# Finer first loads, and two row scales and the MLP norm's squares computed another way, in a one-core hybrid attention layer

## The chip, the core and the metric

The kernel runs on one core of one Trainium2 chip. The metric is the device time of one execution in microseconds; lower is better. The time before is the median of three runs.

## The reference, cut to what matters

One layer over 512 tokens of width 1024 in float32; `rms` is the RMS norm of a token's row times a gain.

```
h    = rms(x);  proj = h @ W_in            # fox q,k,v,f (8 heads of 64), hgrn q,f,i,g (4 heads of 128)
A    = fox_attention(q, k, v, log_sigmoid(f + bias))          # causal, blocks of 128 queries
B    = rms(hgrn2_chunkwise(silu(gq), gf, gi, lb)) * silu(gg)  # gated recurrence
x   += concat(A, B) @ W_out
x   += cross_attention(rms(x), rms(mem)) @ W_xo               # 4 heads, 256 memory tokens
x   += square(relu(rms(x) @ W1)) @ W2                         # width 4096
out  = rms(x)
```

The change touches the row scale 1/sqrt(mean(x^2) + eps) of the first norm and of the MLP's norm, the first loads, and the order in which one projection of the attention is finished.

## The kernel before

**Layout.** Activations are kept feature-major: 8 chunks of 128 features, each with 512 token columns. Every large product is done as three matmuls per chunk of 128: an operand is split into a high part (rounded) and a low part (the rest), and high x high, low x high, high x low are added in PSUM (L240 to L242 in `gemm_fm`). For a panel of weights, ACT rounds the high half (L175, tiles `wh..`) and DVE subtracts it to get the low half (L179, tiles `wl..`); a panel of 256 columns has two halves a and b of four chunks each.

**Row scales are applied late.** The products use the unscaled x times the gain; the scale of a token (a column in this layout) is multiplied in when a product leaves PSUM. For that a vector with one scale per token, held as 128 partitions x 4, must become `rbc`, a tile in which all 128 partitions hold the same 512 scales. Before, PE does it with 4 matmuls of the broadcast vector against the identity (`rbc`, L520 for the first norm, L1500 for the MLP's, 4 of 128 columns; the trace counts two passes of each, 8), and DVE copies the result from PSUM (L522, L1501).

**The first projection.** SP loads x (`xt`, L328) and the first panel (`wr0a`, `wr0b`, L195) in turn, two chunks of weights per load. PE passes the time with matmuls on zeros (`warm`, L352, 7 of them, and L447, 4 more), transposes the chunks of x (`xn`, L412), ACT and DVE write the high and low parts (`hn_hi` L415, `hn_lo` L418), and PE adds up two output tiles gf0 and gf1 (L458 for chunk 0, then L240 to L242). Between the chunks a table `jobs` sets what else ACT and DVE do: splits of weights (`first`, `second`), copies of the transposed x to be parked in DRAM (`x_park`, tiles `xT`), and sums of squares by rows (`x_sq`, L435 on ACT, L437 on DVE, results `ms`). ACT's and DVE's order is written out by hand here; elsewhere a scheduler sets the order on ACT, DVE, POOL and SP from due times, and PE's order is always the order of the code. Then come gf2 and gf3 from panel 1, the four gates `sg` (L544), and the four products gq (L572).

**Fill.** During the recurrence and the attention, `fill` feeds pieces of later projections to PE between the dependent steps, by a credit per step. `proj0` is the first of the attention's projections: its product `pk` becomes `ks` (L765) and the low part `kl` (L770), which the first scores `ps` (L929, L930) read. The recurrence has four state steps c = 0 to 3; `k_T(0)` (L823) copies the transposed keys `kt` from PSUM, which the state products `pst` (L841) read.

**The MLP's norm.** `residual` (L1062 to L1070) produces the new x chunk by chunk; for each chunk POOL squares it and adds it to `ssq`, and after the last chunk PE multiplies `ssq` with ones (`pm`, L1080), DVE and POOL make the scale (L1082, L361, L364), PE spreads it (`rbc`, L1500). `to_tok` transposes the new x back to token rows (`ht` L1162, copies to `acc` L1166, L1168), for the last residual. The MLP's first products u (L240 to L242, tiles u000, u001, u010, u011 in group 0) are scaled by `ur` (L1298), squared (L1301) and summed. POOL also adds rows by accumulating DMAs (`wq`, L1238).

Of the kernel before, what the change touches and what calls it, by code (L numbers as in the profile page):

```python
# [30 lines left out]
GF = 5  # L31
WARM, WARM2 = 7, 4
P1, P2, P3, P4, PW = 20, 20, 20, 10, -20
# [9 lines left out]
def emit(  # L43
# [138 lines left out]

    def load_unit(name, spec, ks, parts=1, between=None):
# [6 lines left out]
        nk = uk // parts  # L190
        splits = []
        for q in range(parts):
            qs, src_ks = slice(q * nk, (q + 1) * nk), slice(ks.start + q * nk, ks.start + (q + 1) * nk)
            for sl, src in spec:
                nc.sync.dma_start(raw_[:, qs, sl], src[:, src_ks, :])  # L195
            if between is not None:
                between(q)
            splits.append(split_of(hi[:, qs, :], lo[:, qs, :], raw_[:, qs, :]))
        return (hi, lo), splits

    def load_next(parts=2, between=None):

        i = len(stream)
        if i >= len(specs):
            return []
        units, splits = [], []
        uk = specs[i][0][1].shape[1] // 2
        for n in range(2):
            note = None if between is None else (lambda q, n=n: between(n * parts // 2 + q))
            unit, some = load_unit(f"{i}{'ab'[n]}", specs[i], slice(n * uk, (n + 1) * uk), parts // 2, note)  # L210
# [118 lines left out]

    def more_x(q):  # L330
        if q == 0:
            load_x(P, P)
        if q < 3:
            load_x((q + 1) * WT)

# [106 lines left out]
    with tc.manual_schedule(engines={mybir.EngineType.Activation, mybir.EngineType.DVE}):  # L442
# [26 lines left out]
        def l_soft():  # L469
# [43 lines left out]
        rstd_of(ms0, NT, "r0", r0)  # L513

        fb = cp.tile([P, FH], F32, name="fb")
        gp.tensor_copy(fb[:, 0:NT], r0)
        gp.dma_start(fb, fox_f_bias[0].partition_broadcast(P))
# [6 lines left out]
        gfps.append(mm("gf3"))  # L524
        gf3 = gemm_fm(gfps[3], wt1, P, hn_hi, hn_lo)
# [27 lines left out]
        x_park(6)  # L553
        gate(0)
        gate(1)
        x_park(5)
        third[0]()
        third[1]()
        run_now(gf3)
        gate(2)  # L560
        for h in range(3):
# [267 lines left out]
    for c in range(NT):  # L829
# [24 lines left out]
        with ahead(P1):  # L854
# [184 lines left out]
    def residual(src_hi, src_lo, g, dst_hi, dst_lo, name, ssq, order, nlast, after=None):  # L1039
# [16 lines left out]
        def rest():  # L1056
            for c in range(KC):
# [6 lines left out]
                ve.scalar_tensor_tensor(dst_lo[:, c, :], hc, g[:, c : c + 1], f(dst_hi[:, c, :]), op0=ALU.mult, op1=ALU.subtract)  # L1064
                if c == 0:
# [93 lines left out]
    def to_tok(c):  # L1159
# [3 lines left out]
        for tb in range(NT):  # L1163
            d, s_ = acc[tb][:, c * P : (c + 1) * P], ps[:, tb * P : (tb + 1) * P]
            if tb % 2 == 0:
                ac.activation(d, s_, AF.Copy)  # L1166
            else:
                ve.tensor_copy(d, s_)  # L1168

    fill.add(x_proj(1), "xq1")  # L1170
    fill.run(2.0)
    for h in range(4):
        if 0 < h < 3:
            fill.add(x_proj(h + 1), f"xq{h + 1}")
        elif h == 3:
            x2_hi, x2_lo = act_tile("x2_hi"), act_tile("x2_lo")
            ssq2 = t2("ssq2")
            early, rest = residual(o_hi, o_lo, g_ff, x2_hi, x2_lo, "xw", ssq2, range(KC), 2, to_tok)
            fill.add(early())
# [324 lines left out]
    for up in ups:  # L1504
        square(*up)
# [44 lines left out]
```

## Time and profile before

| | |
|---|---|
| median of 3 runs | 769.62 us (769.13 to 769.89) |
| the profiled execution's own time | 769.81 us |
| its span in the trace | 768.1 us, 1.7 us less |
| busy PE | 757.7 us, 99% of the span |
| busy DVE, ACT, POOL | 525.1, 368.2, 191.5 us |

The span is what the trace covers; the rest of the profiled execution's time, 1.7 us, lies around it. PE's clock was granted in full, on average 0.999. PE's matmuls stand back to back, so that a stretch of PE work is read best from the chain of work that ended last, where each piece is the time to the next piece.

### The profile page before, as it was taken

What the parts mean: (1) busy time and instruction counts of PE and PEld (TensorE: products, weight loads), DVE (VectorE), ACT (ScalarE), POOL (GpSimd) and SP (SyncE); (2) the same over time, 40 slices, a digit from 0 to 9 for tenths busy, and PEclk for the clock granted to TensorE, in tenths of its full rate; (3) what the DMA queues carried; (4) which work ended last, traced back from release to release, by engine and by line L of the source; (5) the groups of instructions that cost most, each with busy time, mean ns of one, the idle gap of its engine ahead of it and who ended that gap; (6) DMA issues with size and microseconds to landing.
All of it is one profiled execution on the core that took longest, in us unless ns stands there. A gap on an engine that the chain in (4) does not pass through costs nothing.

```text
span 768.1 us, 10959 instructions
## 1 busy us (share of the span) xinstructions
PE 757.7 (99%) x4085; PEld 637.6 (83%) x4085; DVE 525.1 (68%) x847; ACT 368.2 (48%) x618; POOL 191.5 (25%) x264
## 2 busy tenths in 40 slices
PE   8999999999999999999999999999999999999996
PEld 6889888888889988888888888888888888888885
DVE  5747862686867656555548656949596877777696
ACT  5655555665766433244444244435353534342553
POOL 7207531532432125310016510100001010101123
PEclk9999999999999999999999999999999999999999
DMA  8541333231643542222113596565748475758602
GB/s 247 192 124 58 97 84 111 83 98 68 193 158 117 165 135 85 82 92 75 55 55 105 204 257 143 145 161 173 183 146 203 138 191 144 192 137 216 140 1 109
DMA packets 78870, 103.01 MB, mean 134 GB/s; under 512 B 4657, under 2 KB 56410, under 8 KB 78818
## 3 DMA queue, kind: packets, MB, share of 16 engines
q1 hardware_dynamic: 69266, 76.61, 31.2%
q0 software_dynamic: 8960, 24.67, 15.2%
q10 hardware_dynamic: 592, 1.05, 0.4%
q8 instruction: 32, 0.52, 0.3%
q14 instruction: 20, 0.16, 0.1%
HBM read 89.71 MB, written 4.21 MB: 122 GB/s over the span
## 4 chain that ended last, share of the span: by engine, by line
PE 96%; DVE 1%; DMA 1%; POOL 1%; issue 0%; ACT 0%; SPq 0%; POOLq 0%; ACTq 0%
PE u L242 8%; PE u L240 8%; PE u L241 8%; PE U L1364 4%; PE U L1362 4%; PE U L1363 4%; PE xq L240 2%; PE xq L241 2%; PE xw L240 2%; PE xq L242 2%; PE xw L241 2%; PE xw L242 2%; PE wo L240 2%; PE Y L1364 2%; PE wo L242 2%; PE Y L1363 2%
## 5 line engine op out<-in xcount | busy, mean ns | idle before, releaser
L179 DVE TENSOR_TENSOR wld<-wq,whd 128x1024 fp32r<-128x1024 f32 x56 | 68.7, 1226 | 25.5 <-ACT whd L175 25.4
L240 PE MATMUL u<-x_hi,whu 128*128 128x512 f32 x192 | 74.7, 389 | 0.0
L241 PE MATMUL u<-x_lo,whu 128*128 128x512 f32 x192 | 74.7, 389 | 0.0
L242 PE MATMUL u<-x_hi,wlu 128*128 128x512 f32 x192 | 74.7, 389 | 0.0
L175 ACT ACTIVATE whd<-wq 128x1024 fp32r<-128x1024 f32 x56 | 58.4, 1054 | 30.4 <-PE u L241 18.4
L175 ACT ACTIVATE whu<-wru 128x1024 fp32r<-128x1024 f32 x24 | 25.3, 1054 | 61.7 <-DMA wru<-in_w_dram 61.7
L1238 POOL DMA_DIRECT2D wq<-in_w_dram x16 | 19.4, 1242 | 129.6 <-DMA wq<-in_w_dram 118.0
L179 DVE TENSOR_TENSOR wlu<-wru,whu 128x1024 fp32r<-128x1024 f32 x24 | 29.5, 1229 | 32.5 <-ACT whu L175 32.5
L1362 PE MATMUL U<-whd,hb 128*128 128x512 f32 x120 | 46.7, 389 | 0.0
L1363 PE MATMUL U<-wld,hb 128*128 128x512 f32 x120 | 46.7, 389 | 0.0
L1364 PE MATMUL U<-whd,hb 128*128 128x512 f32 x120 | 46.7, 389 | 0.0
L1238 POOL DMA_DIRECT2D wq<-wq x16 | 14.1, 879 | 123.4 <-DVE wld L179 86.3
L241 PEld LDWEIGHTS u<-x_lo,whu 128*128 128x128 f32 x192 | 36.0, 188 | 7.5
L242 PEld LDWEIGHTS u<-x_hi,wlu 128*128 128x128 f32 x192 | 36.0, 188 | 7.5
L240 PEld LDWEIGHTS u<-x_hi,whu 128*128 128x128 f32 x192 | 36.0, 188 | 7.4
L920 POOL TENSOR_SCALAR bi<-nF,Ft 128x128 f32<-128x128 f32 (+3 forms) x32 | 19.6, 620 | 58.2 <-PE pt L952 32.0
L1301 ACT ACTIVATE sq<-ur 128x512 f32<-128x512 f32 x32 | 20.0, 627 | 26.5 <-DVE ur L1298 26.5
L1298 DVE SCALAR_TENSOR_TENSOR ur<-u,rbc 128x512 f32<-128x512 f32 x32 | 21.9, 688 | 11.7 <-PE u L242 11.7
L1363 PEld LDWEIGHTS U<-wld,hb 128*128 128x128 f32 x120 | 22.5, 188 | 4.7
L1364 PEld LDWEIGHTS U<-whd,hb 128*128 128x128 f32 x120 | 22.5, 188 | 4.7
L1362 PEld LDWEIGHTS U<-whd,hb 128*128 128x128 f32 x120 | 22.5, 188 | 4.6
L1063 ACT ACTIVATE x_hi<-hT,gv 128x512 fp32r<-128x512 f32 x16 | 11.5, 719 | 29.3 <-DVE hT L1062 29.3
(960 smaller groups left out, 2313.8 us busy)
## 6 DMA issues: line engine op xcount, KB each, us to landing
wq<-in_w_dram SPq DMA_DIRECT2D x40, 512.0 KB, 3.3
wru<-in_w_dram SPq DMA_DIRECT2D x24, 512.0 KB, 6.5
wq<-in_w_dram POOLq DMA_DIRECT2D x16, 512.0 KB, 8.1
wq<-wq POOLq DMA_DIRECT2D x16, 512.0 KB, 4.7
xTd<-xT POOLq DMA_DIRECT2D x4, 512.0 KB, 3.3
nF<-Fd POOLq DMA_DIRECT2D x8, 256.0 KB, 3.7
hT<-xTd POOLq DMA_DIRECT2D x4, 512.0 KB, 3.6
xt<-in_x_dram SPq DMA_DIRECT2D x3, 512.0 KB
```

Of the source, the lines that this page charges most:

```text
L175: ac.activation(hi, raw, AF.Copy)
L179: ve.tensor_tensor(lo, raw, f(hi), ALU.subtract)
L240: te.matmul(ps, wh, hi, start=n_ == 0 and not begun, stop=False)
L241: te.matmul(ps, wh, lo, start=False, stop=False)
L242: te.matmul(ps, wl, hi, start=False, stop=k == order[-1])
L920: gp.tensor_scalar(bi[:, 0:n], fF[h][:, 0:n], -1.0, Ft[:, tb, h : h + 1], op0=ALU.mult, op1=ALU.add)
L1238: gp.dma_start(raw.rearrange("p (k n) -> p k n", k=2), src, accum_op=ALU.add)
L1298: ve.scalar_tensor_tensor(u, ps, 0.0, rbc2, op0=ALU.max, op1=ALU.mult)
L1301: ac.activation(sqs[g, j][:, i, :], u, AF.Square)
L1362: te.matmul(ps, hi, whi[:, k, :], start=begin, stop=False, skip_group_check=True)
L1363: te.matmul(ps, hi, wlo[:, k, :], start=False, stop=False, skip_group_check=True)
L1364: te.matmul(ps, lo, whi[:, k, :], start=False, stop=k == 1, skip_group_check=True)
```

## The change

Five things are changed.

- **First loads.** Chunks 0 to 3 of x and of panel 0 come one chunk per load, alternating; then chunks 4 and 5 of the weights, then of x, and 6 and 7 likewise: 12 loads where there were 9. The matmuls on zeros are 5 and 2 where they were 7 and 4. The table `jobs` is shifted: the second half of the b splits comes one step later, `x_sq(2)` moves behind the last chunk's `hn_lo`.
- **First row scale.** It no longer goes through PE. POOL writes r0 (16 bytes per partition) to a DRAM tile `Rd`, and reads it back to all partitions as one row of 512 (`on_all`); DVE reorders the row into `rbc`. Gates 0 and 1 come after that copy, behind gf3's products. gf3 and gq0 take PSUM tiles from another pool (`tr`), and the load of the bias `fb` is issued later.
- **The recurrence and the attention.** `kt` of step 0 is copied by DVE instead of ACT. `proj0` is finished before state step 3, by `fill.until`.
- **The MLP's norm.** The squares are taken by token rows from `acc`: four ACT squares of 512 columns at chunk 3, and four DVE reductions of 256 columns each at chunks 5 and 7. The 16 POOL squares and additions and PE's `pm` are gone. The scale goes through `Rd` by two DMAs on ACT's queue.
- **The MLP's first group.** All four u come in one loop behind that; u011 takes its bank from another pool.

```diff
-WARM, WARM2 = 7, 4
+WARM, WARM2 = 5, 2
...
+    xs_ = [*(lambda c=c: load_x(c * P, P) for c in range(1, 4)), lambda: None, lambda: load_x(2 * WT), lambda: load_x(3 * WT)]
...
-    first = load_next(4, more_x)
+    first = load_next(((1, 1, 1, 1), (2, 2)), more_x)
...
+    def on_all(q, i, r, dst):
+        q.dma_start(Rd[i].rearrange("(p t) -> p t", t=NT), r)
+        row = t2(f"row{i}")
+        q.dma_start(row, Rd[i].partition_broadcast(P))
+        def here():
+            ve.tensor_copy(dst.rearrange("p (t q) -> p t q", t=NT), row.rearrange("p (q t) -> p t q", t=NT))
+        return here
...
         jobs = (
-            (first[1],),
-            (lambda: x_park(0), lambda: x_park(1), first[2]),
-            (first[3], lambda: second.extend(load_next())),
-            (lambda: x_sq(0), lambda: x_park(3)),
-            (lambda: x_park(2), lambda: second[0]("h"), lambda: x_sq(2)),
-            (lambda: x_sq(1), lambda: second[0]("l"), lambda: x_sq(3)),
+            (first[2], first[3]),
+            (lambda: x_park(0), lambda: x_park(1)),
+            (first[4], lambda: second.extend(load_next())),
+            (first[5], lambda: x_sq(0), lambda: x_park(3)),
+            (lambda: x_park(2), lambda: second[0]("h")),
+            (lambda: x_sq(1), lambda: x_sq(2), lambda: second[0]("l"), lambda: x_sq(3)),
...
-        pb = sc("rbc")
-        for tb in range(NT):
-            te.matmul(pb[:, tb * P : (tb + 1) * P], r0[:, tb : tb + 1].to_broadcast([P, P]), ident, start=True, stop=True)
-        ve.tensor_copy(rbc, pb)
+        rbc_here = on_all(gp, 0, r0, rbc)
...
-        ac.activation(kts[c], pk, AF.Copy)
+        if c == 0:
+            ve.tensor_copy(kts[c], pk)
+        else:
+            ac.activation(kts[c], pk, AF.Copy)
...
+        if c == NT - 2:
+            fill.until("proj0")
...
+        if c == 3:
+            for tb in range(NT):
+                ac.activation(t2(f"ms2j{tb}"), acc[tb][:, 0:S], AF.Square, scale=1.0 / 32.0, accum_out=ms2[c][:, tb : tb + 1])
...
+            ve.tensor_tensor_reduce(out=t2(f"ms2j{c}{tb}")[:, 0 : 2 * P], in0=a, in1=a, scale=1.0 / D, scalar=old, op0=ALU.mult, op1=ALU.add, accum_out=new_)
...
-    ms2 = mean_sq(ssq2, "pm2")
-    r2 = rstd_of(ms2, NT, "r2")
     to_tok(KC - 2)
     to_tok(KC - 1)
-    up1 = next(ups)
-    pb = tr("rbc2")
-    for tb in range(NT):
-        te.matmul(pb[:, tb * P : (tb + 1) * P], r2[:, tb : tb + 1].to_broadcast([P, P]), ident, start=True, stop=True)
-    ve.tensor_copy(rbc2, pb)
-    square(*up0)
-    square(*up1)
-    for up in ups:
+    gp.tensor_tensor(r2, ms2[KC - 1], mhalf[:, 0:NT], op=ALU.pow)
+    on_all(ac, 1, r2, rbc2)()
+    first_adds(0)
+    for up in [up0, *ups]:
         square(*up)
```

The order on DVE at the end of the first projection, first before, then after. The `ISA` rows are the two parts of one sum of squares by rows (`x_sq`); `wl1a` is the low part of the first half of panel 1, which gf2 reads.

```order
L418 SCALAR_TENSOR_TENSOR hn_lo<-xn_309,g_mix,hn_hi 128x512
L437 ISA x0j_319,ms_193<-xt 128x1024
L437 ISA ms_193 128x1
L418 SCALAR_TENSOR_TENSOR hn_lo<-xn_327,g_mix,hn_hi 128x512
L179 TENSOR_TENSOR wl1a<-wr1a,wh1a 128x1024
```

```order
L430 SCALAR_TENSOR_TENSOR hn_lo<-xn_313,g_mix,hn_hi 128x512
L430 SCALAR_TENSOR_TENSOR hn_lo<-xn_329,g_mix,hn_hi 128x512
L449 ISA x0j_338,ms_195<-xt 128x1024
L449 ISA ms_195 128x1
L179 TENSOR_TENSOR wl1a<-wr1a,wh1a 128x1024
```

One sum of squares has moved from ahead of the last chunk's low part to the place between it and `wl1a`.

The order on DVE at the start of the attention, first before, then after. `rec` is the output of a state step of the recurrence, `mx_lo` the low part of a mixed output, `mt` the memory's rows, `ks` and `kl` the attention's first keys.

```order
L179 TENSOR_TENSOR wl11a<-wr11a,wh11a 128x1024
L862 SCALAR_TENSOR_TENSOR rec_1599<-po_1577,hr_1597,gg_826 128x128 x4
L816 SCALAR_TENSOR_TENSOR mx_lo<-pr_1620,gv,mx_hi 128x4x128
L372 TENSOR_TENSOR m1m<-m1m 128x1
L765 TENSOR_TENSOR ks_1633<-pk_1513,rbc 128x512
L374 TENSOR_SCALAR mt_1607<-mt_1607,m1r 128x1024
L179 TENSOR_TENSOR wl11b<-wr11b,wh11b 128x1024
L770 TENSOR_TENSOR kl_1510<-ks_1633,kh_1509 64x512 x2
```

```order
L179 TENSOR_TENSOR wl11a<-wr11a,wh11a 128x1024
L776 TENSOR_TENSOR ks_1577<-pk_1515,rbc 128x512
L179 TENSOR_TENSOR wl11b<-wr11b,wh11b 128x1024
L781 TENSOR_TENSOR kl_1512<-ks_1577,kh_1511 64x512
L827 SCALAR_TENSOR_TENSOR mx_lo<-pr_1589,gv,mx_hi 128x4x128
L781 TENSOR_TENSOR kl_1512<-ks_1577,kh_1511 64x512
L876 SCALAR_TENSOR_TENSOR rec_1642<-po_1620,hr_1640,gg_828 128x128 x4
```

`ks` and `kl` now stand ahead of the last state step's `rec` and of `mt`, where they stood behind both.

The order on ACT at the MLP's norm, first before, then after. `acc` are the token rows of the last two chunks, `wh36a` and `wh36b` the high halves of a weight panel of the MLP, `sq` the squares of the first u.

```order
L1166 ACTIVATE acc_4211<-ht_4541 128x128
L1166 ACTIVATE acc_4211<-ht_4550 128x128
L175 ACTIVATE wh36a<-wr36a 128x1024
L175 ACTIVATE wh36b<-wr36b 128x1024
L1301 ACTIVATE sq_4592<-ur_4590 128x512
```

```order
L1184 ACTIVATE acc_4212<-ht_4526 128x128
L1184 ACTIVATE acc_4212<-ht_4535 128x128
L175 ACTIVATE wh36a<-wr36a 128x1024
L370 DMA Rd<-r_4553 128x4
L372 DMA row_4556<-Rd 128x512
L175 ACTIVATE wh36b<-wr36b 128x1024
L1338 ACTIVATE sq_4650<-ur_4648 128x512
```

The two DMAs of the scale stand between the two halves of panel 36 on ACT, and the second can be issued only when the first has landed.

## Rows read from the trace of the kernel before

**Rows 1.** The page's busy time by engine: us, share of the span, instructions.

```profile
PE 757.7 (99%) x4085; PEld 637.6 (83%) x4085; DVE 525.1 (68%) x847; ACT 368.2 (48%) x618; POOL 191.5 (25%) x264
```

**Rows 2.** All waits of PE: waiting line, releaser, us, times, longest us.

```profile
PE warm L352 <- DVE ones L356: 1.3, 1, 1.3
PE ps L930 <- DVE kl L770: 1.1, 2, 0.6
PE gf L458 <- DVE wh0a L177: 0.6, 1, 0.6
PE pst L841 <- ACT kt L823: 0.4, 1, 0.4
```

**Rows 3.** Timeline of PE, start: start us, us, what [idle before <-releaser].

```profile
1.29 3.17 PE L352 MATMUL warm<-zero 128*128 128x512 bf16 x7 [1.29 <-DVE ones L356]
...
5.45 1.03 PE L447 MATMUL warm<-zero 128*128 128x512 bf16 x4
7.11 0.70 PE L458 MATMUL gf<-hn_hi,wh0a 128*128 128x512 f32 x2 [0.63 <-DVE wh0a L177]
```

**Rows 4.** Chain that ended last, start: start us, us, what.

```profile
1.29 5.14 DMA wr0a<-in_w_in_dram
```

**Rows 5.** Timeline of ACT in the first projection.

```profile
5.65 0.69 ACT L415 ACTIVATE hn_hi<-xn,g_mix 128x512 fp32r<-128x512 f32 x1 [2.70 <-PE xn L412]
...
14.27 0.62 ACT L175 ACTIVATE wh0b<-wr0b 128x512 fp32r<-128x512 f32 x1
...
18.40 1.06 ACT L175 ACTIVATE wh1a<-wr1a 128x1024 fp32r<-128x1024 f32 x1
19.34 0.69 ACT L415 ACTIVATE hn_hi<-xn,g_mix 128x512 fp32r<-128x512 f32 x1
```

**Rows 6.** Timeline of DVE at the end of the first projection.

```profile
18.72 1.21 DVE L437 CUSTOM_DVE_ANT_0 x0j<-xt 128x1024 f32<-128x1024 f32 x1
...
20.07 0.75 DVE L418 SCALAR_TENSOR_TENSOR hn_lo<-xn,g_mix,hn_hi 128x512 fp32r<-128x512 f32 x1
20.73 1.22 DVE L179 TENSOR_TENSOR wl1a<-wr1a,wh1a 128x1024 fp32r<-128x1024 f32 x1
```

**Rows 7.** Timeline of PE: the first matmul that reads wl1a.

```profile
22.59 0.39 PE L242 MATMUL gf<-hn_hi,wl1a 128*128 128x512 f32 x1
```

**Rows 8.** Chain that ended last: the row scales and the last transposes.

```profile
25.70 0.96 PE rbc L520 x8
...
437.42 0.79 PE pm L1080 x8
438.20 0.93 PE ht L1162 x8
...
444.61 0.89 PE rbc L1500 x8
```

**Rows 9.** Timeline of POOL: the first scale.

```profile
24.37 1.08 POOL L364 TENSOR_TENSOR r<-r0e,mhalf 128x4 f32<-128x4 f32 x1
```

**Rows 10.** The page's DMA issues: queue, form, count, KB each, us to landing.

```profile
wq<-in_w_dram POOLq DMA_DIRECT2D x16, 512.0 KB, 8.1
...
nF<-Fd POOLq DMA_DIRECT2D x8, 256.0 KB, 3.7
...
out_dram<-fo ACTq DMA_DIRECT2D x4, 256.0 KB, 2.3
...
fb<-in_fox_f_bias_dram POOLq DMA_DIRECT2D x1, 4.0 KB, 2.9
```

**Rows 11.** Timeline of DVE: beside kt, and the keys kl.

```profile
126.33 0.16 DVE L372 TENSOR_TENSOR m0m<-m0m 128x1 f32<-128x1 f32 x1 [5.25 <-ACT m0j L371]
...
154.44 2.06 DVE L770 TENSOR_TENSOR kl<-ks,kh 64x512 fp32r<-64x512 f32 x2
```

**Rows 12.** Timelines of DVE and PE: one step of the attention.

```profile
220.49 0.60 DVE L944 TENSOR_SCALAR bi<-bi,dn 128x256 f32<-128x256 f32 x2
...
222.81 0.60 PE L952 MATMUL pt<-ident,bi 128*128 128x128 f32 x4
```

More of the change, by code (lines that the diff above doesn't have):

```diff
@@ L181, in split_of, with load_unit @@
         return split
-    def load_unit(name, spec, ks, parts=1, between=None):
+    def load_unit(name, spec, ks, cuts=None, between=None):
         nw = max(sl.stop for sl, _ in spec)
@@ L189, in load_unit @@
         raw_ = raw_.rearrange("p (k n) -> p k n", k=uk)
[L190 to L193, printed above, removed]
+        splits, q0 = [], 0
+        for nk in cuts or (uk,):
+            qs, src_ks = slice(q0, q0 + nk), slice(ks.start + q0, ks.start + q0 + nk)
+            q0 += nk
             for sl, src in spec:
@@ L196, in load_unit, with load_next @@
             if between is not None:
-                between(q)
+                between()
             splits.append(split_of(hi[:, qs, :], lo[:, qs, :], raw_[:, qs, :]))
         return (hi, lo), splits
-    def load_next(parts=2, between=None):
+    def load_next(cuts=(None, None), between=None):
         i = len(stream)
@@ L208, in load_next @@
         for n in range(2):
-            note = None if between is None else (lambda q, n=n: between(n * parts // 2 + q))
-            unit, some = load_unit(f"{i}{'ab'[n]}", specs[i], slice(n * uk, (n + 1) * uk), parts // 2, note)
+            unit, some = load_unit(f"{i}{'ab'[n]}", specs[i], slice(n * uk, (n + 1) * uk), cuts[n], between)
             units.append(unit)
@@ L328, in load_x, with more_x @@
         nc.sync.dma_start(xt[:, :, gs], x[:, gs].rearrange("(t p) n -> p t n", p=P))
[L330 to L334, printed above, removed]
+    xs_ = [*(lambda c=c: load_x(c * P, P) for c in range(1, 4)), lambda: None, lambda: load_x(2 * WT), lambda: load_x(3 * WT)]
+    def more_x():
+        xs_.pop(0)()
     load_x(0, P)
@@ L365, in rstd_of @@
         return r
+    Rd = drp.tile([2, S], F32, name="Rd")
+    def on_all(q, i, r, dst):
[5 more added lines that the diff above has]
+        return here
     def norm_rows(t, name):
@@ L451, in emit @@
         first[0]("l")
+        first[1]()
         wt0 = stream[0]
@@ L513, in emit @@
         rstd_of(ms0, NT, "r0", r0)
-        fb = cp.tile([P, FH], F32, name="fb")
-        gp.tensor_copy(fb[:, 0:NT], r0)
-        gp.dma_start(fb, fox_f_bias[0].partition_broadcast(P))
-        pb = sc("rbc")
-        for tb in range(NT):
-            te.matmul(pb[:, tb * P : (tb + 1) * P], r0[:, tb : tb + 1].to_broadcast([P, P]), ident, start=True, stop=True)
         rbc = cp.tile([P, S], F32, name="rbc")
-        ve.tensor_copy(rbc, pb)
+        rbc_here = on_all(gp, 0, r0, rbc)
         run_now(gf2)
-        gfps.append(mm("gf3"))
+        gfps.append(tr("gf3"))
         gf3 = gemm_fm(gfps[3], wt1, P, hn_hi, hn_lo)
@@ L553, in emit @@
         x_park(6)
-        gate(0)
-        gate(1)
         x_park(5)
+        fb = cp.tile([P, FH], F32, name="fb")
+        gp.tensor_copy(fb[:, 0:NT], r0)
+        gp.dma_start(fb, fox_f_bias[0].partition_broadcast(P))
         third[0]()
@@ L559, in emit @@
         run_now(gf3)
+        rbc_here()
+        gate(0)
+        gate(1)
         gate(2)
@@ L1064, in rest @@
                 ve.scalar_tensor_tensor(dst_lo[:, c, :], hc, g[:, c : c + 1], f(dst_hi[:, c, :]), op0=ALU.mult, op1=ALU.subtract)
-                if c == 0:
+                if ssq is None:
+                    pass
+                elif c == 0:
                     gp.tensor_tensor(ssq, hc, hc, op=ALU.mult)
@@ L1168, in to_tok, with tok_squares @@
                 ve.tensor_copy(d, s_)
+        if c in (3, 5, 7):
+            tok_squares(c)
+    ms2 = {}
+    def tok_squares(c):
+        if c == 3:
+            ms2[c] = sm(NT, "ms2")
+            for tb in range(NT):
+                ac.activation(t2(f"ms2j{tb}"), acc[tb][:, 0:S], AF.Square, scale=1.0 / 32.0, accum_out=ms2[c][:, tb : tb + 1])
+            gp.tensor_scalar(ms2[c], ms2[c], 1.0, EPS, op0=ALU.mult, op1=ALU.add)
+            return
+        cs = slice((c - 1) * P, (c + 1) * P)
+        ms2[c] = sm(NT, f"ms2{c}")
+        for tb in range(NT):
+            a, v = acc[tb][:, cs], (x[:, tb : tb + 1] for x in (ms2[c], ms2[c - 2]))
+            new_, old = v
+            ve.tensor_tensor_reduce(out=t2(f"ms2j{c}{tb}")[:, 0 : 2 * P], in0=a, in1=a, scale=1.0 / D, scalar=old, op0=ALU.mult, op1=ALU.add, accum_out=new_)
     fill.add(x_proj(1), "xq1")
@@ L1176, in emit @@
             x2_hi, x2_lo = act_tile("x2_hi"), act_tile("x2_lo")
-            ssq2 = t2("ssq2")
-            early, rest = residual(o_hi, o_lo, g_ff, x2_hi, x2_lo, "xw", ssq2, range(KC), 2, to_tok)
+            early, rest = residual(o_hi, o_lo, g_ff, x2_hi, x2_lo, "xw", None, range(KC), 2, to_tok)
             fill.add(early())
@@ L1471, in mlp_up_group @@
                 if (g, j) == (0, 0):
-                    down_raws(0)
+                    load_raws(0, RAWS)
                 elif (g, j) == (1, 1):
```

5 lines of the change are left out of this document (3 added, 2 removed).

## The prediction

> **What bounds the kernel now.** I read the busy time by engine first [rows 1]: PE works 757.7 of 768.1 us, and no other engine is above 68%. So time can go in two ways only: work leaves PE, or one of PE's few idle stretches closes. Then the list of PE's waits [rows 2]: four entries, 3.4 us in all, of which 1.3 is the start of the program, which the change leaves alone. The other three, gf 0.6, ps 1.1 and pst 0.4, are each touched by a part of the change. Then the chain of work that ended last [rows 8], in which each piece of PE's work is as long as the time until the next piece: there stand the passes that only make a row scale, 0.96 us, 0.79 us and 0.89 us. Last I read the timelines of ACT and DVE around these places [rows 5, 6, 11, 12], for what is late next.
>
> **The first scale's matmuls.** The 8 passes of `rbc` leave PE: 0.96 us [rows 8]. In their place r0, ready at 24.37 + 1.08 = 25.45 [rows 9], goes through two DMAs on POOL's queue. The nearest rows are fb, 4 KB in pieces of 32 bytes, 2.9 us, and nF, a 256 KB broadcast, 3.7 us [rows 10]. So the row is there at about 25.45 + 0.65 to issue + 2.9 + 0.65 + 3.7 = 33.4, DVE's copy ends at about 34.1, gates 0 and 1 leave gf0's and gf1's banks by about 35.5. What hides it: PE has gf2, gf3 and gq0 to do, each 24 matmuls; one such tile takes 444.61 - 439.13 = 5.48 us [rows 8], and gf2 begins two matmuls ahead of the one at 22.59 [rows 7], at about 22.1. So a bank is needed again at 22.1 + 3 x 5.48 = 38.5, 3 us after. At the 8.1 us that POOL's queue took for large loads [rows 10] for the two it would be 25.45 + 1.3 + 16.2 + 2.1 = 45.1, 6.6 us too late; the transfers are no such loads, so I take no wait, with 0 to 1 as bounds. Worth -0.96.
>
> The row of fb says 2.9 us for a load in small pieces, less than a large broadcast. The Trainium skill, "DMA: Bandwidth & Descriptors", section "Specifications", speaks against this part: below 512 bytes a DMA engine reads, modifies and writes, and does not reach line rate; here the pieces are 16 bytes. Its section "Anatomy of one DMA — SWDGE (gpsimd) path" gives some 2.0 us fixed for each DMA, by which each of the two would take 2.0 to 2.6 us, an estimate, and the row would be there 2 us sooner than in my sum. By the first rule it would be there later, which is rival (e); the row of fb, at 32 bytes, does not bear that out.
>
> **kt on DVE.** PE waits 0.4 us for ACT's copy [rows 2], which stands behind a sum of squares. DVE sits idle for 5.25 us before 126.33 [rows 11], so it takes kt as soon as PE has written it. -0.39, bounds 0 and -0.4.
>
> **proj0 ended sooner.** PE waits 1.1 us for `kl` [rows 2], 2.06 us of DVE work that starts at 154.44 behind a scaling of the memory rows and a weight split [rows 11]. With `pk` complete before state step 3, `ks` and `kl` come ahead of that step's outputs on DVE, and the wait goes: -1.07. What is late next: the pieces of pk that stood beside the attention's first step are used up, so every later step of the attention meets the fill some ten matmuls (2.3 us) later than before, and the weight splits and `ks` on DVE stand at other places among the softmax steps. The cover there is thin: in one step DVE's last scaling ends at 220.49 + 0.60 = 221.09, and PE transposes it at 222.81 [rows 12], 1.7 us of slack, while one weight split on DVE takes 1.22 [rows 6] and `ks` as much as one more 128x512 pass, about 0.7. Where both go ahead of the scaling the slack is 1.7 - 1.9 = -0.2, a wait of 0.2 us. After also has no fill left between the last weighted sum and the output projection. Some four steps look like this, so I take +0.7; bounds 0 (all covered) and +1.5.
>
> **The MLP's norm.** Off PE go `pm`, 0.79, and `rbc`, 0.89 [rows 8]: -1.68. `ht` stays. Its cover: `ht` ends at 438.20 + 0.93 = 439.13; then come copies to `acc`, four reductions of 256 columns on DVE, POOL's power 1.08 [rows 9], two DMAs on ACT's queue, the copy and the first `ur`. The reductions are bounded by 4 x 1.21 = 4.8 (a whole row of 1024 each, [rows 6]) and a quarter of that; I take 2.5 with the copies. The DMAs are bounded by 2.3 (ACT's queue) and 3.7 (a broadcast) each [rows 10], I take 2.9 + 3.7; copy and `ur` 0.7 each. Sum 439.13 + 2.5 + 1.1 + 6.6 + 1.4 = 450.7. PE needs u000's bank only after u001, u010 and u011, at 439.13 + 3 x 5.48 = 455.6: 4.9 us of slack; at the upper ends (4.8 and 3.7 + 3.7) it is 1.8. Queued behind ACT's waiting DMA issue is the high half of panel 36b, which PE needs only in the next group; POOL, free of 16 square passes, has its accumulating DMAs ahead of the power, which costs at most their issue. So no wait, and 0 to 1 as bounds.
>
> **The start.** PE waits 0.63 us for the first cast [rows 2, 3], which waits for a load of two chunks that landed 5.14 us after it began [rows 4]. With one chunk per load the cast is no longer last; `hn_hi`, 5.65 + 0.69 = 6.34 [rows 5], is, and gf can start at about 6.45 instead of 7.11. That is a gain of 0.66 there, and up to 1.0 with the small gaps for x behind it. But PE then runs into gf2, whose third matmul reads `wl1a`, at 22.59 [rows 7]. The changed order puts a sum of squares, 1.21 us, between the last `hn_lo` and `wl1a` [rows 6], and on ACT a weight split of 0.62 is moved behind the later chunks, in a row of work that already leaves little room: `wh1a` from 18.40, the last `hn_hi` from 19.34 [rows 5]. If that `hn_hi` starts 0.5 us earlier than before, at 18.85, then `hn_lo` runs 19.55 to 20.3, the squares to 21.45, `wl1a` to 22.6, and PE goes on at about 22.7: 0.1 later than before, so the whole gain is given back. I take +0.1; bounds -1.0 (wl1a in time) and +0.8 (ACT no earlier than before: `hn_lo` at 20.07, `wl1a` done 1.2 us later than the 21.95 of before, at 23.2, and some of the lost time in the last chunk too).
>
> **Sum.** -0.96 - 0.39 - 1.07 + 0.7 - 1.68 + 0.1 = -3.3 us. The profiled execution took 769.81, 0.19 above the median of 769.62; its own time would become 766.5, the median 766.3.
>
> **The rivals.** (a) The start keeps its gain: ACT and DVE are far enough ahead that `wl1a` is in time, -1.0 instead of +0.1, 765.2. For it: the last `hn_hi` needs only to start 1.4 us earlier than its 19.34 [rows 5] for that. Against it: the 1.21 of squares in front of `wl1a`, and ACT's split that has moved behind. Chance 0.15.
>
> (b) The clock. The 7 matmuls on zeros took 0.45 us each, the 4 later ones 0.26 [rows 3]: the first are at the lower level of 1.2 GHz, the later at 2.4 GHz. With 5 and 2, PE does less before 6.4, and the first chunk's products could still run at the lower level: 6 matmuls at 0.45 instead of 0.26, and one chunk more, about +2 us at the place, of which the wait for `wl1a` would swallow 0.6 to 1.0, so about +1.1, 767.4. Chance 0.12. The Trainium skill, "TensorE: Matmul & The Clock Gate", section "What's actually happening", says the throttled state is the default and that activity releases it, which the two durations agree with.
>
> (c) The attention pays the upper end, +1.5 instead of +0.7, and a little more at its last step, +0.6: 767.7. For it: the thin slack [rows 12]. Chance 0.12.
>
> (d) The other side: the MLP's scale is late. If the two small DMAs on ACT's queue, which start while the MLP's 512 KB loads are running, take 8.1 us each as POOL's loads of that stretch [rows 10], the row scale is ready at 439.13 + 2.5 to 4.8 + 1.1 + 16.2 + 1.4 = 460.3 to 462.6, and PE, which wants the bank at 455.6, stands for 4.7 to 7.0 us: about 772. The change loses as soon as the two take over 6.6 + 4.9 + 3.3 = 14.8 us. Against it: 2.3 us on ACT's queue at the end. Chance 0.05.
>
> (e) The first stage's bank is late: the small pieces make each of POOL's two DMAs take 6 us, between 3.7 and 8.1 [rows 10]. Then the bank is free at 25.45 + 1.3 + 12 + 2.1 = 40.9, 2.4 us after 38.5: 768.7. The 2.9 us of fb speaks against it. Chance 0.03.
>
> **How the numbers follow.** The forecast, 766.3, has 0.53. What a measurement here can tell from no change is 0.2%, 1.5 us, so faster means below 768.1. The forecast, (a), most of (b) and half of (c) fall there: 0.53 + 0.15 + 0.10 + 0.06 = 0.84. Within are the rest of (b) and (c) and (e): 0.02 + 0.06 + 0.03 = 0.11. Slower is (d), 0.05. The range: downward (a) with no wait in the attention, 765.2 - 0.7 = 764.5, of which I leave out the last part, 764.9; upward the forecast with the bounds of the start and the attention, 766.3 + 0.8 + 0.8 = 767.9, and (c), 768.2. Outside remain (d), (e), and some of (a) and (c), about 0.18.
>
> **What would show it.** In the changed kernel's chain no `rbc` and no `pm`; among PE's waits no `kl` and no `kt`; the first gf at about 6.45 and a new wait of PE for `wl1a`, about 1 us, in gf2; some short waits of the attention's transposes for DVE's scaling; none at the gates and none of u for `ur`. If PE's busy time doesn't fall by about 2.6 us, the matmuls' price was wrong; if a wait for `ur` or a gate stands in the list, the DMAs' price was.

## The result and the profile after

The changed kernel takes **771.31 us** (median of 12 runs, 767.88 to 772.82) where the kernel before took 769.46 (12 runs, 769.12 to 770.90): ratio 1.002, 95% interval 1.0011 to 1.0030, 1.85 us slower. The forecast was 766.3, its range 764.9 to 768.2, and it gave a slower kernel a chance of 0.05. The profiled execution took 770.80; its span is 769.1. Two of the twelve runs took 767.88 and 768.72, with a mean granted clock of 0.998 where the others had 0.996; no trace was taken of them.

The page's busy times by engine, which answer to [rows 1]:

```profile
PE 756.1 (98%) x4057; PEld 635.6 (83%) x4057; DVE 519.1 (67%) x865; ACT 369.3 (48%) x627; POOL 171.9 (22%) x251
```

PE is busy 1.6 us less, and yet the span is 1.0 longer. The forecast wanted 2.6 less; some 1.6 of busy time came back in slow matmuls, which are shown below. (The POOL passes that are gone are 15, not 16: one square for chunk 0, a square and an addition for each of the other seven.) The list of PE's waits (waiting line, releaser, us, times, longest), which answers to [rows 2]:

```profile
PE u L239 <- DVE ur L1335: 2.7, 1, 2.7
PE warm L351 <- DVE ones L355: 1.3, 1, 1.3
PE pt L968 <- DVE bi L960: 0.7, 1, 0.7
PE dg L653 <- DVE z L620: 0.4, 1, 0.4
PE gf L241 <- DVE wl1a L179: 0.4, 1, 0.4
PE gf L471 <- ACT hn_hi L427: 0.3, 1, 0.3
```

The waits for kl and kt are gone, as forecast, and wl1a stands in the list, as forecast. The first line was not in the forecast: it is the wait of rival (d). The chain of work that ended last, around the MLP's norm (start us, us, what), shows why PE stands there:

```profile
435.60 0.87 PE ht L1180 x8
...
442.47 6.67 DMA Rd<-r
...
449.22 4.79 DMA row<-Rd
...
454.03 0.63 DVE rbc L375
...
454.68 0.70 DVE ur L1335
...
455.52 0.77 PE u L239
456.29 0.43 PE u L240
456.71 0.43 PE u L241
...
458.42 0.38 PE u L239
458.80 0.23 PE u L240
```

From the end of `ht` at 436.47 to the end of `ur` at 455.39 are 18.9 us; I had counted 11.6. And behind the wait each matmul takes 0.43 us instead of 0.23, until 458.4. The table of busy time by stretch (stretch: us, then each engine's busy us and instructions, granted clock, DMA share, GB/s) has the clock's side of it:

```profile
452.00:454.00 2.00, 0.81 (x4) 0.35 (x2) 0.00 (x0) 0.00 (x0) 0.07 (x1) 1.00 0.56 164
...
456.00:457.00 1.00, 1.00 (x4) 0.72 (x3) 0.57 (x1) 0.97 (x3) 0.00 (x0) 0.50 1.12 306
...
458.00:459.00 1.00, 1.00 (x4) 0.78 (x4) 0.23 (x2) 1.00 (x2) 0.93 (x1) 0.70 1.04 190
459.00:460.00 1.00, 1.00 (x6) 0.81 (x5) 1.00 (x2) 0.71 (x1) 0.27 (x1) 1.00 0.17 27
```

PE stood from about 452.65 to 455.52; then the granted clock is 0.50, the 1.2 GHz level, with PE busy without a gap, and 1.00 again by 459. Seven matmuls take 458.80 - 455.52 = 3.28 us, where seven at 0.23 take 1.61.

The account by place, from when the same piece of PE's work starts in the two traces (negative: the changed kernel is ahead):

| piece of PE's work | before | after | after - before | what it shows |
|---|---|---|---|---|
| gf, first matmul with wl1a | 22.59 | 22.07 | -0.52 | the start keeps half a us |
| gq, first | 34.02 | 32.64 | -1.38 | `rbc` is gone |
| gi, last | 125.17 | 124.45 | -0.72 | 0.66 lost at dg |
| pst, first | 126.84 | 125.57 | -1.27 | no wait for kt |
| xq, first | 314.94 | 313.12 | -1.82 | no wait for kl, 0.7 for pt |
| chunk 7's ht | 438.20 | 435.60 | -2.60 | `pm` is gone |
| u's second panel, half b | 448.10 | 444.49 | -3.61 | the second `rbc` is gone |
| u of the next group | 456.26 | 455.52 | -0.74 | 2.9 lost for ur |
| last product Z | 758.18 | 759.00 | +0.82 | 1.6 lost to the clock |

PE's timeline before, first at the account's row 7 and then at its row 8, and after at its row 7 (start us, us, what; row 8 of after stands in the chain above):

```profile
448.10 0.39 PE L240 MATMUL u<-x_hi,wh35b 128*128 128x512 f32 x1
...
456.26 0.39 PE L240 MATMUL u<-x_hi,wh36a 128*128 128x512 f32 x1
```

```profile
444.49 0.39 PE L239 MATMUL u<-x_hi,wh35b 128*128 128x512 f32 x1
```

In these two traces the changed kernel was 3.61 us ahead up to the wait for `ur`; the forecast's whole sum was 3.3. All of the trace's loss, 4.4, stands in one place, and the forecast had put it at nothing. The two profiled executions are 0.99 us apart and the medians 1.85, so 0.9 of the difference stands in no row of the account.

### The profile page after: what moved, and what is told of

Its sections match the earlier page's. It is cut to its first block, busy times and chain, and to the rows that moved or that the text cites. A ratio compares the mean times of both kernels' runs of the same rounds, so it can differ in the third digit from the quotient of the medians.

```text
span 769.1 us, 10909 instructions
## 1 busy us (share of the span) xinstructions
PE 756.1 (98%) x4057; PEld 635.6 (83%) x4057; DVE 519.1 (67%) x865; ACT 369.3 (48%) x627; POOL 171.9 (22%) x251
## 4 chain that ended last, share of the span: by engine, by line
PE 87%; DMA 4%; ACT 3%; DVE 3%; issue 2%; POOL 1%; SPq 0%; ACTq 0%; POOLq 0%; DVEq 0%
PE u L239 7%; PE u L240 7%; PE u L241 7%; PE U L1401 4%; PE U L1399 4%; PE U L1400 4%; PE xq L239 2%; PE wo L239 2%; PE xq L240 2%; PE xq L241 2%; PE xw L240 2%; PE xw L241 2%; PE wo L241 2%; PE xw L239 2%; PE Y L1401 2%; PE Y L1400 2%
## 5 line engine op out<-in xcount | busy, mean ns | idle before, releaser
L936 POOL TENSOR_SCALAR bi<-nF,Ft 128x128 f32<-128x128 f32 (+3 forms) x32 | 22.7, 717 | 58.4 <-PE pt L968 34.0
L1355 ACT ACTIVATE hb<-s 128x512 fp32r<-128x512 f32 x24 | 15.0, 630 | 20.7 <-PE U L1401 13.7
```

The source lines that it names most:

```text
L936: gp.tensor_scalar(bi[:, 0:n], fF[h][:, 0:n], -1.0, Ft[:, tb, h : h + 1], op0=ALU.mult, op1=ALU.add)
```

## The experiments

Each edit is against the kernel named; all were timed beside the kernel before on the same chip, and "against before" is the difference of those medians.

**e1: the scale on PE, the squares by rows kept** (edit of the changed kernel).

```diff
-    on_all(ac, 1, r2, rbc2)()
+    up1 = next(ups)
+    up2 = next(ups)
+    pb = tr("rbc2")
+    for tb in range(NT):
+        te.matmul(pb[:, tb * P : (tb + 1) * P], r2[:, tb : tb + 1].to_broadcast([P, P]), ident, start=True, stop=True)
+    ve.tensor_copy(rbc2, pb)
     first_adds(0)
-    for up in [up0, *ups]:
+    for up in [up0, up1, up2, *ups]:
```

> The changed kernel, but the MLP's row scale is spread over the partitions by PE's 4 matmuls again, behind the third tile u; the squares by rows stay. Theory: the scale through DRAM comes late, PE stands 2.7 us for ur and then runs at the lower clock level for 7 matmuls, 4.4 us in all. Then this kernel has no wait for ur, pays about 0.9 for the matmuls, and takes 771.3 - 4.4 + 0.9 = 767.8. Rival: the squares by rows or the moved banks cost the time; then the wait stays in another form and the time stays at 770 or above.

Measured: 767.62, ratio 0.998 (0.9971 to 0.9989), 1.71 under before, and no wait for ur in its trace. The time lies with the way through DRAM, not with the squares.

**e2: POOL's power ahead of its accumulating DMAs** (edit of the changed kernel).

```diff
-    gp.tensor_tensor(r2, ms2[KC - 1], mhalf[:, 0:NT], op=ALU.pow)
+    with tc.manual_schedule(engines={mybir.EngineType.Pool}):
+        gp.tensor_tensor(r2, ms2[KC - 1], mhalf[:, 0:NT], op=ALU.pow)
+        first_adds(0)
     on_all(ac, 1, r2, rbc2)()
-    first_adds(0)
```

> The changed kernel, with POOL's power of the MLP's scale ahead of its two accumulating DMAs instead of behind. Theory (the chain is simply too long by 2.9 us, of which POOL's order makes about 2.2): PE's wait shrinks to about 0.7, the clock doesn't fall, about 767.7. If the write of the scale took 6.7 us because the accumulating DMAs were issued just ahead of it, it falls to about 3, no wait at all, 766.9. Rival: the accumulating DMAs now start beside the write and slow it as much; the wait stays at 1.5 to 3, 769 to 771.

Measured: 769.17, ratio 1.000 (0.9992 to 1.0009), 0.16 under before; the wait for ur is 1.6. In the changed kernel POOL's timeline reads as follows; the power stands behind the two DMAs' issue and takes 1.64 instead of the 1.08 of [rows 9]:

```profile
438.82 2.56 POOL L1274 DMA_DIRECT2D wq<-in_w_dram  x2 [21.68 <-DVE ms L1205]
440.81 1.64 POOL L1533 TENSOR_TENSOR r<-ms,mhalf 128x4 f32<-128x4 f32 x1
```

The chain of e2, with the power first:

```profile
440.56 1.05 POOL r L1534
...
441.63 5.26 DMA Rd<-r
...
446.96 7.33 DMA row<-Rd
```

The theory and its rival each have a share: the scale starts earlier against `ht` and the write is shorter by 1.4, but the broadcast, beside which the accumulating DMAs now run, takes 2.5 longer. The time is the rival's, 769 to 771. In this trace the clock stayed up after a wait of 1.6: the stretch from 456 to 457 reads

```profile
456.00:457.00 1.00, 1.00 (x5) 0.82 (x5) 0.85 (x2) 0.97 (x3) 0.72 (x1) 1.00 0.66 254
```

The trace speaks for eight of e2's eleven runs, with a mean granted clock of 0.998 or 0.999 and 768.24 to 769.67 us; three have 0.996, as most runs of the changed kernel, and 770.46 to 771.71.

**e3: power first, accumulating DMAs held until the row scale is there** (edit of the changed kernel).

```diff
-    gp.tensor_tensor(r2, ms2[KC - 1], mhalf[:, 0:NT], op=ALU.pow)
-    on_all(ac, 1, r2, rbc2)()
-    first_adds(0)
+    held = sm(1, "held")
+    with tc.manual_schedule(engines={mybir.EngineType.Pool}):
+        gp.tensor_tensor(r2, ms2[KC - 1], mhalf[:, 0:NT], op=ALU.pow)
+        on_all(ac, 1, r2, rbc2)()
+        gp.tensor_copy(held, rbc2[:, 0:1])
+        first_adds(0)
```

> The changed kernel, with the power first and the two accumulating DMAs held until the row scale is there, so that they run beside neither DMA of the scale. If the 16-byte pieces themselves make the write slow, it still takes 6 us or more; if the accumulating DMAs do, it takes about 2.6 as in the first stage, and the broadcast about 3.7: the scale is ready about 7 us sooner than in the changed kernel, no wait, 766.9; if the weight loads of SP's queue do, it lies between, 4 to 6, and PE waits for less than 0.5.

Measured: 766.86, ratio 0.9966 (0.9953 to 0.9978), 2.47 under before, no wait for ur. ACT's timeline with the two issues, and then DVE's with the copy that waits for the row:

```profile
440.93 0.36 ACTq L370 DMA_DIRECT2D Rd<-r  x1
445.95 0.33 ACTq L372 DMA_DIRECT2D row<-Rd  x1
```

```profile
449.51 0.62 DVE L375 COPY rbc<-row 128x512 f32<-128x512 f32 x1 [0.79 <-DMA row<-Rd]
```

The write takes 5.0 still, the broadcast 3.6. So with the power first and the accumulating DMAs held the two are about 1.7 and 1.2 shorter than in the changed kernel; what is left of the write's time it takes beside SP's weight loads alone.

**e4: the whole MLP norm as before** (edit of the changed kernel: `tok_squares`, the row scale through DRAM and u011's bank undone).

```diff
...
+    ms2 = mean_sq(ssq2, "pm2")
+    r2 = rstd_of(ms2, NT, "r2")
...
-    gp.tensor_tensor(r2, ms2[KC - 1], mhalf[:, 0:NT], op=ALU.pow)
-    on_all(ac, 1, r2, rbc2)()
-    first_adds(0)
...
+        te.matmul(pb[:, tb * P : (tb + 1) * P], r2[:, tb : tb + 1].to_broadcast([P, P]), ident, start=True, stop=True)
```

> The changed kernel with the whole MLP norm as before (squares on POOL, sums and scale on PE). Theory: all other parts keep what the trace shows ahead of the last transposes, PE 1.8 us earlier than before: 769.5 - 1.8 = 767.7. Rival: what is gained ahead of the MLP is lost again behind it, as weight loads and buffers set the end: 769.0 or above.

Measured: 768.68, ratio 0.9993 (0.9984 to 1.0001), 0.65 under before, and the interval just takes in no change: a miss by 1.0. Its trace is 1.3 ahead of before from the cross-attention to the end, so the rival's loss behind the MLP is not there; but its start is 0.6 later than that of the changed kernel's trace (the clock at the start, below), and its own time of 768.68 is 1.1 under that of the profiled execution before, 769.81, which was itself 0.5 above the median of before here. The other parts are worth 0.65 in the medians, not 1.8. From here the MLP's norm, with a scale in time, is worth 2.47 - 0.65 = 1.8 (e3), against 1.68 in the forecast.

**e5: 7 and 4 matmuls on zeros** (edit of e3).

```diff
-WARM, WARM2 = 5, 2
+WARM, WARM2 = 7, 4
```

> The kernel of e3 (adds held), with 7 and 4 matmuls on zeros again instead of 5 and 2. In four of the five profiles with 5 and 2, the second group's matmuls and the first two of gf still take 0.43 to 0.58 us each, the lower level, and PE is some 0.5 to 0.8 us later behind them. Theory: with 7 and 4 the first gf runs at 0.23 to 0.27 us; it starts perhaps 0.3 later; 0.3 to 0.6 faster than e3, 766.4. Rival: PE waits for wl1a in any case, ACT's row of work sets the time, no difference: 766.9.

Measured: 767.25, ratio 0.997 (0.9958 to 0.9983), 2.37 under before: the same as e3 within the spread, the rival. Two timelines of PE at the start, first the changed kernel's, then e3's, show what the theory rested on:

```profile
4.72 0.59 PE L459 MATMUL warm<-zero 128*128 128x512 bf16 x2
5.66 0.73 PE L471 MATMUL gf<-hn_hi,wh0a 128*128 128x512 f32 x2 [0.35 <-ACT hn_hi L427]
```

```profile
4.79 1.06 PE L459 MATMUL warm<-zero 128*128 128x512 bf16 x2
5.77 1.22 PE L471 MATMUL gf<-hn_hi,wh0a 128*128 128x512 f32 x2
```

The start of the two programs is the same; it runs at the full level in one trace and at the lower level in the other, as rival (b) had it. The granted clock of the profile's rows reads 1.00 in both stretches, so it is the lengths that tell. In e5's own trace the first two gf take 0.73.

**e6: the third sum of squares of x behind wl1a** (edit of e3).

```diff
-            (lambda: x_sq(1), lambda: x_sq(2), lambda: second[0]("l"), lambda: x_sq(3)),
+            (lambda: x_sq(1), lambda: second[0]("l"), lambda: x_sq(2), lambda: x_sq(3)),
```

> The kernel of e3, with the third sum of squares of x behind the low part wl1a on DVE instead of ahead of it, nothing else. Theory: PE's wait for wl1a (0.4 in the list, 0.5 with the restart) goes, the first scale is as late as before: 0.5 faster than e3, 766.4. Rival: the row of work on ACT and DVE is late anyway, or the scale's chain comes later: 766.9 or above.

Measured: 766.71, ratio 0.9964 (0.9951 to 0.9976), 2.91 under before, with no wait for wl1a left in its list. It is 0.44 better against before than e3, as expected, though the spreads of the two overlap. Its trace doesn't decide more: it began at the full clock level (0.74 for the first two gf), e3's at the lower. With e10 it has the lowest median of the series, under both kernels'.

**e7: the first scale on PE again** (edit of e3: `on_all` for r0, the gates' place and the banks undone).

```diff
...
+        pb = sc("rbc")
+        for tb in range(NT):
+            te.matmul(pb[:, tb * P : (tb + 1) * P], r0[:, tb : tb + 1].to_broadcast([P, P]), ident, start=True, stop=True)
         rbc = cp.tile([P, S], F32, name="rbc")
-        rbc_here = on_all(gp, 0, r0, rbc)
+        ve.tensor_copy(rbc, pb)
...
```

> The kernel of e3, with the first norm's row scale on PE again (matmuls, gates and banks as before). Theory: the detour through DRAM makes the gates and behind them the weight splits and loads some 3.5 us late, which PE pays with about 0.65 at the recurrence's first products (dg); so the detour is worth only 0.96 - 0.65 = 0.3: 767.2, and no wait for z or Ac. Rival: the wait at dg is not of the detour; then it stays and the time is 767.8.

Measured: 767.19, ratio 0.9971 (0.9959 to 0.9982), 2.43 under before; e3 was 2.47 under. Its list has no wait for z, and another that is new:

```profile
PE rbc L533 <- POOL r L363: 0.2, 1, 0.2
```

So the wait at dg belongs to the way through DRAM, with the gates and banks that were moved for it. From the first gq to the last gi PE takes 91.15 us before and 91.14 in e7, 91.81 in the changed kernel and 91.70 in e3. The way is worth nothing that these runs can tell, not 0.96.

**e8: the scale in four pieces of 512 bytes** (edit of e3).

```diff
-        on_all(ac, 1, r2, rbc2)()
...
+        rp = tr("rp", (P,))[0:NT, :]
+        te.transpose(rp, r2, ident)
+        rs = t2("rs", F32, (P,))[0:NT, :]
+        ve.tensor_copy(rs, rp)
+        ac.dma_start(Rd[1].rearrange("(t q) -> t q", t=NT), rs)
...
```

> The kernel of e3, but PE transposes the MLP's scale first (one matmul), and it is written to DRAM in 4 pieces of 512 bytes instead of 128 of 16. In e3 the write took 5.0 us beside SP's weight loads, with no accumulating DMA. If the small pieces make it long, it takes 2 to 3 us now; if it waits behind the loads in flight, it takes 4 to 6 again. No wait of PE either way, about 767.0.

Measured: 768.50, ratio 0.9983 (0.9975 to 0.9992), 1.12 under before, with a wait for ur of 1.9 that nobody expected. The chain of e8:

```profile
434.59 9.89 DMA wr36b<-in_w_dram
...
444.67 3.71 DMA Rd<-rs
...
448.45 5.77 DMA row<-Rd
```

ACT's order had come out with the split of panel 36b ahead of the two issues, and that split waits for a load that took 9.9 us. One accumulating DMA also ran beside the broadcast. The write took 3.7 us, between the two expectations and at another moment than in e3: on the pieces' size the run decides nothing.

**e9: PE's wait filled** (edit of the changed kernel; the added products are read by nobody).

```diff
     for up in [up0, *ups]:
         square(*up)
+    spare = pvt("spare")
+    for _ in range(12):
+        te.matmul(spare, x2_hi[:, 0, 0:P], x2_hi[:, 0, :], start=True, stop=True)
```

> The changed kernel, with 12 matmuls of 512 columns, whose result nobody reads, on PE between the last tile u of the first group and the tile that waits for ur. PE would stand there for about 2.7 us anyway. Theory: the clock falls because PE stands; with the wait filled it stays at the full level, and the 7 slow matmuls behind it (0.43 instead of 0.23 us each, 1.35 in all) go: 771.3 - 1.35 = 770.0, with the wait for ur still some 0 to 0.5 after the spare ones. Rival: the lower clock there has another reason, the time stays at 771.3 or grows by the spare matmuls.

Measured: 770.00, ratio 1.001 (1.0001 to 1.0019), 0.66 over before, where the changed kernel is 1.85 over. PE's timeline, and then the stretch behind from the table by stretch, with the granted clock third from the end:

```profile
453.18 2.88 PE L1540 MATMUL spare<-x_hi 128*128 128x512 f32 x12
455.90 0.39 PE L239 MATMUL u<-x_hi,wh36a 128*128 128x512 f32 x1
456.13 0.39 PE L240 MATMUL u<-x_lo,wh36a 128*128 128x512 f32 x1
```

```profile
456.00:457.00 1.00, 1.00 (x6) 0.84 (x5) 0.49 (x1) 0.97 (x2) 0.00 (x0) 1.00 1.19 250
```

Against before, twelve useless matmuls made the kernel 1.2 us faster. The scale is as late (the copy to `rbc` starts at 453.95, in the changed kernel at 454.03), and the next tile starts 0.4 us later, but runs at 0.23 a matmul. The clock's share of the loss is shown: it fell because PE stood.

**e10: the MLP's scale on POOL's queue** (edit of e3).

```diff
-        on_all(ac, 1, r2, rbc2)()
+        on_all(gp, 1, r2, rbc2)()
```

> The kernel of e3 (adds held), with the two DMAs of the MLP's scale on POOL's queue instead of ACT's. If ACT's queue, beside SP's loads, makes the write of 2 KB take 5.0 us, it takes about 2.6 here, as in the first stage; if the loads in flight make it long whatever the queue, 4 to 6 again. No wait of PE either way, 766.9.

Measured: 766.69, ratio 0.9966 (0.9953 to 0.9978), 2.65 under before. POOL's timeline:

```profile
441.32 0.62 POOL L370 DMA_DIRECT2D Rd<-r  x1 [0.29 <-POOL r L1535]
446.54 0.55 POOL L372 DMA_DIRECT2D row<-Rd  x1 [4.60 <-DMA Rd<-r]
```

From issue to issue 5.2 us, as on ACT's queue: it is not the queue. The same write of 128 pieces of 16 bytes on POOL's queue took 2.63 in the first stage of the changed kernel, by its chain:

```profile
25.81 2.63 DMA Rd<-r
```

The DMA engines' share in the changed kernel there and at the MLP's norm (last but one number):

```profile
25.80:28.50 2.70, 2.70 (x13) 2.23 (x13) 2.42 (x4) 1.28 (x3) 1.93 (x4) 1.00 0.60 179
...
442.50:449.10 6.60, 6.60 (x31) 5.47 (x30) 0.00 (x0) 0.00 (x0) 0.00 (x0) 1.00 1.07 233
```

So what goes with the longer time is the load on the DMA engines. The two transfers of a scale at seven places of the traces, each with the mean DMA share while it was under way (its own part included):

| run and place | write: us, DMA share | broadcast: us, DMA share |
|---|---|---|
| changed kernel, first stage | 2.6, 0.60 | 5.9, 0.93 |
| e8, MLP (4 pieces) | 3.7, 0.71 | 5.8, 1.01 |
| e10, MLP (POOL's queue) | 4.9, 1.00 | 3.9, 0.77 |
| e3, MLP | 5.0, 1.02 | 3.6, 0.58 |
| e2, MLP | 5.3, 0.98 | 7.3, 1.10 |
| e9, MLP | 6.1, 1.10 | 5.0, 0.97 |
| changed kernel, MLP | 6.7, 1.07 | 4.8, 0.85 |

In both columns the time mostly goes up with the share. No run took SP's weight loads away, so their part is read from these rows and not from an edit.

**e11: proj0 finished as before** (edit of e3).

```diff
-        if c == NT - 2:
-            fill.until("proj0")
```

> The kernel of e3, without the call that finishes proj0 ahead of state step 3. The trace of the changed kernel gains 0.47 us between the state steps and the output projection. Theory: without the call PE waits again for kl twice, about 1.1, and no longer for the transposes (0.7): 0.4 to 0.5 slower than e3, 767.3. Rival: the later steps of the attention lose as much as kl gains, no difference: 766.9.

Measured: 767.73, ratio 0.9981 (0.9972 to 0.9990), 1.61 under before, so the call is worth some 0.86, in intervals that overlap; the traces say the same: from the first pst to the first xq PE takes 188.40 us here and 187.54 in e3. The wait for kl is back, longer than in [rows 2], and that for pt is gone:

```profile
PE ps L944 <- DVE kl L781: 1.5, 2, 0.9
```

**e12: e5 and e6 together** (edit of e6: 7 and 4).

> The kernel of e6 (adds held, third sum of squares behind wl1a), with 7 and 4 matmuls on zeros. In e5 the 7 and 4 changed nothing, since PE then waited for wl1a; with that wait gone the first chunks' pace should reach the rest. Theory: the first gf starts 0.4 later (6.18 instead of 5.77), but never at the lower clock level, which costs 0.5 to 0.8 where it happens: about 0.2 faster than e6, 766.5, and a narrower spread. Rival: ACT's row of work sets the pace either way: 766.7, spread as before.

Measured: 766.93, ratio 0.997 (0.9958 to 0.9982), 2.25 under before, 766.46 to 767.27. Not faster than e6; the spread, 0.8 against 1.4 us, is narrower, on six and five runs. In its trace the first gf started at 6.63, not at 6.18. The rival's time holds.

## Why the prediction was wrong, step by step

**The step that failed: the cover of the MLP's norm.** The forecast said that the scale would be ready 4.9 us before PE needs u000's bank, and at the upper ends 1.8. It was 2.9 late, 7.8 us worse than my value. The terms, from the end of `ht`, by the rows above:

| term | forecast | measured |
|---|---|---|
| copies and reductions | 2.5 (1.2 to 4.8) | 2.7 |
| POOL's power | 1.1 | 3.3 with the issues ahead of it |
| write of the scale | 2.9 (2.3 to 3.7) | 6.7 |
| broadcast of the row | 3.7 (2.3 to 3.7) | 4.8 |
| copy and ur | 1.4 | 1.3 |

Two things went wrong with the durations. The prices of the small DMAs came from rows where the DMA engines had room: fb from the first stage, `out_dram` from the end. The row that belongs to this place was the one of POOL's 512 KB loads, 8.1 [rows 10], and the page of before has a DMA share of nine tenths or more in the slice from 441.7 to 460.9 us, the 24th of the 40 digits of this row:

```profile
DMA  8541333231643542222113596565748475758602
```

I read 8.1 as the price of large transfers and gave it to rival (d) alone; the table under e10 shows that the same 2 KB takes 2.6, or 5 to 6.7 with the load. And the forecast said that POOL's accumulating DMAs cost "at most their issue" and then put that issue at nothing: it is 2.56 for the two, on an engine that the scale needs next, by POOL's row under e2, and the power itself took 0.6 longer there. Of the 7.3 us by which the chain from `ht` was longer, the two transfers have 4.9 and POOL 2.2.

The Trainium skill, "DMA: Bandwidth & Descriptors", section "Anatomy of one DMA — SWDGE (gpsimd) path", gives about 2.0 us fixed per DMA and a term for the bytes. The 2.63 of the first stage is near that; the 4.9 of the same transfer on the same queue in e10 is not, and there the measurement decides. The rule on pieces under 512 bytes that the prediction cites from this page of the Trainium skill remains open here: at 0.60 of DMA share 128 pieces of 16 bytes took no more than 2.6, and e8 could not compare the two sizes under one load.

**The price of the wait.** Rival (d) counted the time that PE stands and no more: the change was to lose as soon as the two transfers took over 14.8 us. They took 11.5, and it lost. POOL's issue had used up part of the slack, and standing for 2.7 us also cost 1.6 behind it in the trace, 1.2 by e9's median; a wait of 1.6 cost nothing behind it in e2's trace. That made the loss in the trace 4.4 instead of 2.9, and in the medians it is the larger part of what the changed kernel is over before: 1.85 with it, 0.66 without (e9). So rival (d)'s "about 772" is near the 771.31 by luck: it had the place, not the terms.

**What the forecast had right.** The prices of the matmuls: `rbc` 0.96, `pm` 0.79, `rbc` 0.89; the account by place has 0.86, 0.78 and 1.01 there. kt: -0.55 against -0.39. The attention: -0.55 in the account against -0.37, with the wait for kl gone and a new wait of 0.7 for DVE's scaling, which runs at 163.69, behind `ks` from 162.90: that was the mechanism. That its size was the forecast's is luck: it is one wait in the attention's first step, where I had counted some four of 0.2. The call alone is worth -0.86 by e11. The last weighted sum made no wait. That the trace was 3.61 ahead at the wait and the forecast's sum was 3.3 is luck too: in the medians the kernel with the scale in time, e3, is 2.47 under before.

**The start.** The mechanism held: PE ran into wl1a, the wait is 0.4, and DVE's sum of squares stood in front (e6). Its size in the trace was -0.42 (the -1.38 at gq without the 0.96 of `rbc`), not +0.1: the first gf began at 5.66, not 6.45, and the last `hn_hi` at 18.27, not 18.85. But this trace began at the full clock level, and others of the same start did not (e5). The whole of the parts ahead of the MLP measures -0.65 (e4), where the forecast had -1.6, so part of that gain is absent in the median.

**The first scale.** The matmuls left, -0.96, and 0.66 came back at dg, which the forecast had put at nothing because it followed only the banks; rival (e), a bank 2.4 us late, is not what happened. What came late was the weights. The row of 512 took 5.9 us instead of 3.7, at a DMA share of 0.93, and behind the copy and the gates stand DVE's and ACT's splits of panel 3. The changed kernel's DVE timeline, and then its chain from the load of panel 4b on:

```profile
34.69 0.62 DVE L375 COPY rbc<-row 128x512 f32<-128x512 f32 x1 [3.98 <-DMA row<-Rd]
...
41.33 1.22 DVE L179 TENSOR_TENSOR wl3a<-wr3a,wh3a 128x1024 fp32r<-128x1024 f32 x1 [2.36 <-ACT wh3a L175]
```

```profile
46.93 4.50 DMA wr4b<-in_w_in_dram
...
58.82 0.89 DVE wl5b L179
...
60.38 0.14 DVE z L620
...
60.52 0.69 PE dg L653 x16
```

Before, wl3a started 3.5 us sooner:

```profile
37.80 1.23 DVE L179 TENSOR_TENSOR wl3a<-wr3a,wh3a 128x1024 fp32r<-128x1024 f32 x1 [2.88 <-ACT wh3a L175]
```

With panel 3 split that much later its buffer comes free later, the load of panel 4b starts later, and two panels on the split wl5b stands just ahead of z. e7 takes the cause away and the wait with it.

**What stays open.** Whether pieces of 512 bytes would shorten the write under load; what SP's weight loads alone cost it; why three of e2's runs have the lower mean clock; how much of the first scale's way is gain in the median (e7 and e3 differ by less than their spreads); and how the two runs of 767.88 and 768.72 differed, other than by their clock.

## What to carry to other kernels

Price a small transfer by the load on the DMA engines at its own place and moment, not by its size or by its fastest row; and where a chain of two such transfers replaces work on the bounding engine, issue no other DMA ahead of it or beside it that can wait. Follow a late value past the buffer that it frees to the next loads: weights that are prefetched late can be paid for two panels on, as here. Where PE must stand as long as here, try spare work in the wait: the clock behind it cost about half as much again as the wait.

## What the runs showed of the hardware that I had not expected

- The landing of a 2 KB write in 128 pieces: 2.6 us at a DMA share of 0.60, 4.9 to 5.0 beside weight loads (e10 on POOL's queue, e3 on ACT's), 5.3 with accumulating DMAs issued just behind it (e2), 6.7 with them issued ahead of it. A 256 KB broadcast: 3.6 us at a DMA share of 0.58, 7.3 at 1.10.
- PE at the 1.2 GHz level (granted clock 0.50) after standing for 2.7 us, at the 2.4 GHz level after standing for 1.6 in e2's trace; 12 useless matmuls in the wait of 2.7 kept it up and saved 1.2 us.
- With 5 and 2 matmuls on zeros at the start, the first two products took 0.73 or 0.74 us together in three traces (the changed kernel, e6, e9) and 0.99 to 1.22 in the others, of the same program up to there.
